# A decoder layer on one core: x for the head's factors in tiles of their own, and w_o's reloads on ScalarE's queue

## The chip, the cores and the metric

The kernel runs on one core of one Trainium2 chip. Work is shared by TensorE (PE in the profile: matmuls and transposes), VectorE (DVE), ScalarE (ACT), GpSimd (POOL, little used here) and SyncE (SP, which only issues DMAs). Each engine carries out its own instructions strictly in order, and waits at the first one whose input or buffer isn't ready. ScalarE can issue DMAs too; then the issue stands in the same order as its computations. The metric is the device time in microseconds (us). The kernel before takes 2449.53 us, the median of three runs (2446.66 to 2450.91).

## The reference

One hybrid decoder layer in float32 on 512 tokens of width 2048:

```python
h = rms_norm(x, g_mix)
z = h @ w_in          # attn q,k,v | ret q,k,v | ret gate, 8 heads of 128 each
a_out = moba_attention(rotary(rms(q)), rotary(rms(k)), v)       # 8 heads, causal
r = retention_chunkwise(rotary(rq), rotary(rk) * 128**-0.5, rv) # 8 heads, decay per head
r_out = silu(rg) * (r * rsqrt(mean(r*r) + eps)) * g_ret
x = x + concat(a_out, r_out) @ w_o
x = x + (silu(h2 @ w_gate) * (h2 @ w_up)) @ w_down              # h2 = rms_norm(x, g_ffn)
x = x + (p @ w_ple_proj) * sigmoid(rms_norm(x, g_ple) @ w_ple_gate + b)
```

## The kernel before

**Number format.** A float32 product is made of three matmuls on a high and a low part: `split` (L51) makes the high part with a copy on ScalarE (H, L54) and the low part with a subtraction on VectorE (L55); `mm3` (L61 to L64) multiplies high by high, high by low and low by high. Weights are split in the same way, into `wh` and `wl` (three buffers each), one unit of 256 rows by 512 columns at a time.

**Products of factors.** Most projections use seven products in place of eight (a Strassen-Winograd scheme, the order of L101 is 1, 5, 6, 3, 7, 2, 4). The weights' sums are made by VectorE (L70), and the other operand's sums, its factors, by `factors` (L155) or, in the head, by `first_factors` (L426). A product goes to one of the PSUM banks X, Y and Z (L125). A unit of a product is 12 matmuls of 512 columns, a product of four units 48.

**The head.** Chunks of x, transposed (128 rows by 512), are loaded by `h_chunk` (L420), multiplied by the gain on ScalarE (L423), and split into the tile `h`. With `h` PE first makes the plain projection of the first q/k pair (class `Plain`, eight units of 24 matmuls, each of which needs two chunks of h). It ends in four copies `z0` out of PSUM (L414). Meanwhile `first_factors(k)` loads two chunks of x again for each of eight k, and makes the sums t (L67) and their splits into the tiles of products 5, 6, 3 and 7. Then the products of the values and gates follow (`groups`, L461): product 1 goes to X, product 5 to Z, which `z0` has to empty first. Besides, 16 tiles `xn` of x are loaded for the sums of squares (`sq`, L486), which the first rms norm needs. The tiles x, xn, sq, z0 and zeros all take turns in four buffers with the tag "o". `beside(i)` (L468) says at which step each piece of this is asked for.

**The middle.** Eight pairs of heads follow: four of attention, four of retention. For a retention pair `qk_ret` (L674) projects q and k (eight units from `h`), copies the four results `zr` out of PSUM (L680), swaps their halves by two small DMAs each on ScalarE's queue (`mr`, L683 and L684), turns them (L686 to L688) and splits them into qkH and qkL. `retain` (L696) makes the heads' output, and `factors` its factors for w_o. These go to DRAM (`spill`, tensors s_mix), since the tiles for w_o take the place of `h`, which lives until the last projection. In the last step of the loop (L751) `h` is given back, the tiles s_o of products 1, 5, 6 and 3 are opened, and `back` (L744) reloads them from DRAM on SP's queue: nine transfers of 512 KB, three of 256 KB and one of 1.75 MB. Then come `retain` for the last pair, whose factors go straight to the tiles, and the projection of p (L782; four units of 24 matmuls, with copies `pp` out of PSUM, L790). It needs pT, which takes the buffer of the table ropeT, free after the last turn.

**What sets the order.** The code gives the order of calls, but the program is laid out by a scheduler which keeps a simulated clock and moves each engine's instructions against each other as far as data and buffers allow. Every DMA issue also takes one of eight completion semaphores in turn, and so waits for the DMA eight before it.

Of the kernel before, what the change touches and what calls it, by code (L numbers as in the profile page):

```python
# [10 lines left out]
F32 = mybir.dt.float32  # L11
F32R = mybir.dt.float32r
BF16 = mybir.dt.bfloat16
AF = mybir.ActivationFunctionType
# [3 lines left out]
P = 128  # L18
# [3 lines left out]
NC = D // P  # L22
NS = D // 512
HD = 128
NPAIR = 4
# [8 lines left out]
def layer_kernel(ctx, tc, x, xT, pT, g_mix, wqk, w_vg, qk_norm, g_ret, w_ow, g_ffn,  # L34
                 w_gu, w_dn, g_ple, w_pl, b_pg, w_pp,
                 ident_c, rope_c, ropeT_c, decay_c, mask_c, out):
    nc = tc.nc
    PSUM = bass.MemoryType.PSUM

    def pool(name, bufs=1, side="left", **kw):  # L40
        return tc.tile_pool(name=name, bufs=bufs, side=side, reuse_waits="tile", **kw)
# [9 lines left out]
    def split(H, L, src, scale=None):  # L51

        if scale is None:
            nc.scalar.activation(H, src, AF.Copy)  # L54
            nc.vector.tensor_tensor(L, src, H.bitcast(F32), op=ALU.subtract)  # L55
        else:
            nc.scalar.activation(H, src, AF.Copy, scale=scale)
            nc.vector.scalar_tensor_tensor(L, src, scale, H.bitcast(F32),
                                           op0=ALU.mult, op1=ALU.subtract)
# [6 lines left out]
    def sub(o, a, b):  # L66
        nc.vector.tensor_tensor(o, a, b, op=ALU.subtract)  # L67
# [7 lines left out]
    def rstd_of(ssq, r):  # L75

        nc.vector.tensor_reduce(r, ssq, axis=AX.X, op=ALU.add)
        nc.vector.tensor_scalar(r, r, 1.0 / D, EPS, op0=ALU.mult, op1=ALU.add)
        power(r, r, NB)
# [23 lines left out]
    def kept(name, n):  # L103
        return {p: dram.tile([P, n + 2 if p == "4" and n == 4 else n, 2, 256], F32R, name=f"{name}_{p}")
                for p in ORDER}

    KG = [8, 8, 6]
    s_mix = kept("mix", 8)
# [23 lines left out]
    pools = {}  # L132

    def later(n, fn):
        due.setdefault(now[0] + n, []).append(fn)
# [16 lines left out]
    def ev_tile(tag, bufs=2, shape=(P, T), name=None, dt=F32):  # L152
        return pools["ev"].tile(list(shape), dt, name=name or tag, tag=tag, bufs=bufs)

    def factors(a0, a1, sink):  # L155

        lo, hi = slice(0, 256), slice(256, 512)
        t = [ev_tile("t", 2, (P, 2, 256)) for _ in range(2)]
        s1, s2, s3, s4 = t[0][:, 0], t[0][:, 1], t[1][:, 0], t[1][:, 1]
        made = {"1": a0[:, lo], "5": s1, "6": s2, "3": s4, "7": s3, "2": a1[:, lo], "4": a1[:, hi]}  # L160
        first = {"5": lambda: sub(s1, a0[:, hi], a1[:, hi]), "6": lambda: sub(s2, a0[:, lo], s1),
                 "3": lambda: sub(s4, a1[:, lo], s2), "7": lambda: sub(s3, a1[:, hi], s2)}
        for p in ORDER:
            if p in first:
                first[p]()
            H, L, end = sink(p)
            split(H, L, made[p])
            end()

    def into(tiles, k):  # L170
        return lambda p: (tiles[p][:, k, 0, :], tiles[p][:, k, 1, :], lambda: None)

    def spill(where, k, wait=1):
        def sink(p):
            o = ev_tile("o", 4, (P, 2, 256), dt=F32R)
            store = lambda: nc.sync.dma_start(where[p][:, k].bitcast(F32), o.bitcast(F32))
            return o[:, 0, :], o[:, 1, :], lambda: later(wait, store) if wait else store()
        return sink

    def factor_tile(p):  # L180
        return pools.get("s" + p, pools["s"]).tile(
            [P, 8, 2, 256], F32R, name="s" + p, tag="s" + p)
# [177 lines left out]
    h_ctx = ctx.enter_context(ExitStack())  # L360
# [14 lines left out]

    zeros = ev_tile("o", 4, name="zeros", dt=BF16)
    nc.vector.memset(zeros, 0.0)
    idle = tp_p.tile([P, T], F32, name="tp", tag="tp")
    for _ in range(10):
        nc.tensor.matmul(idle, zeros[:, :P], zeros, start=True, stop=True)  # L380
# [36 lines left out]
    zd = [dram.tile([P, T], F32, name=f"z_{b}") for b in range(NB)]  # L417
    first = Plain()

    def h_chunk(k):  # L420
        t = ev_tile("o", 4, name="x")
        nc.sync.dma_start(t, xT[k * P:(k + 1) * P, :])
        nc.scalar.activation(t, t, AF.Copy, scale=gm[:, k:k + 1])  # L423
        return t

    def first_factors(k):  # L426

        a = [h_chunk(2 * k + c) for c in range(2)]
        lo, hi = slice(0, 256), slice(256, 512)
        t = [ev_tile("v", name="t", shape=(P, 2, 256)) for _ in range(2)]  # L430
        s1, s2, s3, s4 = t[0][:, 0], t[0][:, 1], t[1][:, 0], t[1][:, 1]
        sub(s1, a[0][:, hi], a[1][:, hi])
        sub(s2, a[0][:, lo], s1)
        split(s_h["5"][:, k, 0, :], s_h["5"][:, k, 1, :], s1)
        split(s_h["6"][:, k, 0, :], s_h["6"][:, k, 1, :], s2)
        sub(s4, a[1][:, lo], s2)
        sub(s3, a[1][:, hi], s2)
        split(s_h["3"][:, k, 0, :], s_h["3"][:, k, 1, :], s4)
        split(s_h["7"][:, k, 0, :], s_h["7"][:, k, 1, :], s3)
# [28 lines left out]
    def beside(i):  # L468

        if -2 <= i < NC // 2 - 2:  # L470
            for k in (2 * i + 4, 2 * i + 5):
                t = h_chunk(k)
                split(h[:, k, 0, :], h[:, k, 1, :], t)
            first.load(i + 2)
        if 3 <= i < 3 + NC // 2:
            first_factors(i - 3)
        for at, q in ((2, "11"), (3, "12"), (6, "22")):
            if i == at:
                for u in range(4):
                    groups[0].load(q, u)  # L480
        if 6 <= i < 22:
            b, s = divmod(i - 6, NS)
            t = ev_tile("o", 4, name="xn")
            nc.sync.dma_start(t, x[b * P:(b + 1) * P, s * T:(s + 1) * T])
            sq = ev_tile("o", 4, name="sq")
            nc.scalar.activation(sq, t, AF.Square, accum_out=ssq[0][:, b, s:s + 1])  # L486
        elif i == 22:
            rstd_of(ssq[0], rstd[0])

    run(beside)  # L490
    s_ctx.close()
    ev_ctx.close()
# [12 lines left out]
    def rm_tile(name, shape=(P, T), dt=F32):  # L505
        return ev2.tile(list(shape), dt, name=name, tag="rm", bufs=4)
# [52 lines left out]
    def load_ropeT():  # L559
        t = ap.tile([P, 2, T], F32, name="ropeT", tag="rope")  # L560
        nc.sync.dma_start(t, ropeT_c)
        bc = rp_tile("bc")
        nc.scalar.activation(bc, over_partitions(rstd1), AF.Copy)
        nc.vector.tensor_tensor(t, t, bc[:, None, :].to_broadcast([P, 2, T]), op=ALU.mult)
        tab[0] = t
# [6 lines left out]
    def v_of(i):  # L572
        v = ap.tile([P, NB, 2, 256], F32R, name="v", tag="v")
        j = i % NPAIR
        for b in range(NB):
            nc.sync.dma_start(v[:, b].bitcast(F32), vd[i // NPAIR][:, b, :, j * 256:(j + 1) * 256].bitcast(F32))
        return v
# [165 lines left out]

    def back(p, pairs):  # L744

        nc.sync.dma_start(s_o[p][:, pairs].bitcast(F32), s_mix[p][:, pairs].bitcast(F32))

    qk, v = qk_attn(0), v_of(0)
    s_o = {}
    for i in range(2 * NPAIR):  # L750
        if i + 1 == 2 * NPAIR:  # L751
            h_ctx.close()
            pools["s"] = ctx.enter_context(pool("s2"))
            s_o.update({p: factor_tile(p) for p in "1563"})
            for u in range(3):
                for p in "156":
                    back(p, slice(2 * u, 2 * u + 2))
            for p in "156":
                back(p, slice(6, 7))
            back("3", slice(0, 7))  # L760
        if i < NPAIR:
            made = [attend(qk, v, j) for j in range(2)]
        else:
            made = [retain(qk, v, j, 2 * (i - NPAIR) + j) for j in range(2)]
        spilled = spill(s_mix, i, 0)
        direct = into(s_o, i)
        factors(*made, lambda p: (direct if p in s_o else spilled)(p))
        if i + 1 < 2 * NPAIR:
            if i + 1 == NPAIR:
                load_ropeT()  # L770
            qk = qk_attn(i + 1) if i + 1 < NPAIR else qk_ret(i + 1)
            v = v_of(i + 1)


    pTH = []
# [6 lines left out]
    for n in range(NS):  # L782
        wh, wl = weights(w_pp[n])
        accs = [acc_p.tile([P, T], F32, name="acc", tag="acc") for _ in range(NB)]
        for b in range(NB):
            at = slice(b * P, (b + 1) * P)
            for c in range(2):
                mm3(accs[b], pTH[c][0][:, at], pTH[c][1][:, at], wh[:, c, :], wl[:, c, :], c == 0, c == 1)
            t = rm_tile("pp")
            nc.scalar.activation(t, accs[b], AF.Copy)  # L790
            nc.sync.dma_start(ppd[b][:, n], t)
    mix_ctx.close()


# [3 lines left out]
    pools["chain"] = ctx.enter_context(pool("chain2", space=PSUM))  # L798
    s_o.update({p: factor_tile(p) for p in "724"})
    for p in "724":  # L800
        back(p, slice(0, 8))

    s_c, s_e = {}, {}
    s_d = [{}, {}, {}]
# [35 lines left out]
    for kg in range(3):  # L840
        for n in range(2):
            after = lambda p: None
            if n == 1:
# [3 lines left out]
                                         lambda tb, s, kg=kg: xd[kg + 1][tb][:, s],  # L847
# [105 lines left out]
```

## Time and profile before

| | |
|---|---|
| time before | 2449.53 us (2446.66 to 2450.91) |
| profiled execution, device time | 2448.14 us |
| its span | 2446.4 us |
| PE busy | 2332.6 us (95%) |
| DVE busy | 1958.1 us (80%) |
| ACT busy | 1211.8 us (50%) |
| mean granted TensorE clock | 0.984 |

The span runs from the first to the last instruction of the trace; the device time holds 1.7 us more. A busy PE is not a PE at its peak, since matmuls overlap: at full clock one of 512 columns starts every 0.227 us and shows 0.39 us. The same holds on DVE and ACT, where the shown duration exceeds the distance of two that follow each other: a subtraction of 128x1024 takes 1.14 us so (shown 1.22), one of 128x512 0.60, one of 128x256 0.34; on ACT a copy of 128x512 about 0.52 to 0.62, one of 128x1024 0.95, one of 128x256 0.31.

### The profile page before, as it was taken

The numbers are of one execution on the slowest core, as the hardware profiler recorded it, in microseconds if no ns is written. First come the engines' busy times: TensorE is split into PE (matmuls) and PEld (weight loads), VectorE is DVE, ScalarE is ACT, GpSimd is POOL, SyncE is SP. The second block draws the span as 40 slices with busy tenths as digits, with TensorE's granted clock in tenths as the row PEclk, the third lists the DMA queues.
The fourth block names the chain that finished last, engine by engine and source line by source line (L and its number), as shares of the span: only waits on it lengthen the run. The fifth ranks groups of instructions, "written<-read, shape, count | busy, mean of one in ns | idle before, by whom it ended". The sixth has DMA issues, their size and how long they took to land.

```text
span 2446.4 us, 29405 instructions
## 1 busy us (share of the span) xinstructions
PE 2332.6 (95%) x10470; PEld 1911.5 (78%) x10470; DVE 1958.1 (80%) x2632; ACT 1211.8 (50%) x1886; POOL 62.4 (3%) x63
## 2 busy tenths in 40 slices
PE   8799999998986998999999999999999999999898
PEld 6578877787875876888888888888877878878677
DVE  5787767766566898798888988899878878789897
ACT  6654534444445465455445554455544434346543
POOL 0000011210000000000000000000000000000000
PEclk9899999999997999999999999999999999999999
DMA  7456453344567768444455444654595676767763
GB/s 277 140 187 206 151 163 116 117 134 141 171 190 251 265 203 308 137 147 128 135 186 176 138 128 156 194 155 132 172 397 180 249 282 209 295 235 242 260 213 121
DMA packets 170291, 469.91 MB, mean 192 GB/s; under 512 B 18848, under 2 KB 31520, under 8 KB 165152
## 3 DMA queue, kind: packets, MB, share of 16 engines
q1 hardware_dynamic: 167440, 463.82, 56.4%
q10 hardware_dynamic: 2704, 4.20, 0.7%
q8 instruction: 82, 1.34, 0.2%
q14 instruction: 65, 0.53, 0.1%
HBM read 357.33 MB, written 106.43 MB: 190 GB/s over the span
## 4 chain that ended last, share of the span: by engine, by line
PE 67%; DVE 10%; DMA 6%; issue 3%; ACT 1%; ACTq 0%; POOL 0%; SPq 0%; DVEq 0%
PE Y L63 8%; PE Y L64 8%; PE Y L62 8%; PE Z L63 5%; PE Z L64 5%; PE Z L62 5%; PE X L63 5%; PE X L64 5%; PE X L62 5%; PE acc L62 4%; PE acc L64 4%; PE acc L63 3%; DVE wl L55 3%; DVE raw L70 2%; DMA mr<-zr 1%
## 5 line engine op out<-in xcount | busy, mean ns | idle before, releaser
L54 ACT ACTIVATE wh<-raw 128x1024 fp32r<-128x1024 f32 x726 | 767.3, 1059 | 801.4 <-PE Y L64 283.2
L55 DVE TENSOR_TENSOR wl<-raw,wh 128x1024 fp32r<-128x1024 f32 x726 | 884.0, 1224 | 273.0 <-ACT wh L54 268.9
L70 DVE TENSOR_TENSOR raw<-raw 128x1024 f32<-128x1024 f32 x376 | 455.5, 1224 | 35.0 <-DMA raw<-in_w_gu 11.3
L63 PE MATMUL Y<-wl,s 128*128 128x512 f32 x1080 | 425.5, 394 | 3.4 <-DVE wl L55 3.2
L64 PE MATMUL Y<-wh,s 128*128 128x512 f32 x1080 | 421.8, 391 | 0.0
L62 PE MATMUL Y<-wh,s 128*128 128x512 f32 x1080 | 379.0, 391 | 9.7 <-ACT wh L54 9.7
L63 PE MATMUL Z<-wl,s 128*128 128x512 f32 x752 | 298.5, 397 | 6.6 <-DVE wl L55 6.6
L64 PE MATMUL Z<-wh,s 128*128 128x512 f32 x752 | 295.1, 393 | 0.0
L62 PE MATMUL Z<-wh,s 128*128 128x512 f32 x752 | 267.4, 395 | 19.6 <-ACT z L414 16.4
L63 PE MATMUL X<-wl,s 128*128 128x512 f32 x656 | 258.3, 394 | 5.9 <-DVE wl L55 5.6
L64 PE MATMUL X<-wh,s 128*128 128x512 f32 x656 | 256.3, 391 | 0.0
L62 PEld LDWEIGHTS Y<-wh,s 128*128 128x128 f32 x1080 | 202.1, 188 | 55.7 <-ACT wh L54 14.0
L63 PEld LDWEIGHTS Y<-wl,s 128*128 128x128 f32 x1080 | 203.3, 188 | 47.7 <-DVE wl L55 6.3
L64 PEld LDWEIGHTS Y<-wh,s 128*128 128x128 f32 x1080 | 203.4, 188 | 41.2
L62 PE MATMUL X<-wh,s 128*128 128x512 f32 x656 | 231.2, 392 | 2.3 <-ACT wh L54 2.3
L62 PEld LDWEIGHTS Z<-wh,s 128*128 128x128 f32 x752 | 141.5, 190 | 50.5 <-ACT z L414 16.8
L63 PEld LDWEIGHTS Z<-wl,s 128*128 128x128 f32 x752 | 142.7, 190 | 40.0 <-DVE wl L55 11.1
L64 PEld LDWEIGHTS Z<-wh,s 128*128 128x128 f32 x752 | 142.6, 190 | 28.8
L63 PEld LDWEIGHTS X<-wl,s 128*128 128x128 f32 x656 | 123.8, 189 | 34.4 <-DVE wl L55 8.9
L62 PEld LDWEIGHTS X<-wh,s 128*128 128x128 f32 x656 | 123.3, 189 | 29.5 <-ACT wh L54 3.9
L64 PEld LDWEIGHTS X<-wh,s 128*128 128x128 f32 x656 | 123.8, 189 | 25.3
L62 PE MATMUL acc<-h,wh 128*128 128x512 f32 x256 | 100.9, 397 | 6.0 <-ACT zr L680 4.0
(207 smaller groups left out, 2821.8 us busy)
## 6 DMA issues: line engine op xcount, KB each, us to landing
raw<-in_w_gu SPq DMA_DIRECT2D x176, 512.0 KB, 4.3
raw<-in_w_dn SPq DMA_DIRECT2D x88, 512.0 KB, 6.1
a<-o SPq DMA_DIRECT2D x154, 256.0 KB, 2.5
raw<-in_wqk SPq DMA_DIRECT2D x64, 512.0 KB, 3.9
s<-a SPq DMA_DIRECT2D x14, 2048.0 KB, 10.8
raw<-in_w_vg SPq DMA_DIRECT2D x48, 512.0 KB, 5.4
raw<-in_w_ow SPq DMA_DIRECT2D x32, 512.0 KB, 4.5
xin<-x SPq DMA_DIRECT2D x64, 256.0 KB, 6.0
```

The lines of the kernel that those rows point to most:

```text
L54: nc.scalar.activation(H, src, AF.Copy)
L55: nc.vector.tensor_tensor(L, src, H.bitcast(F32), op=ALU.subtract)
L62: nc.tensor.matmul(o, aH, bH, start=start, stop=False, skip_group_check=goes_on)
L63: nc.tensor.matmul(o, aH, bL, start=False, stop=False, skip_group_check=goes_on)
L64: nc.tensor.matmul(o, aL, bH, start=False, stop=stop, skip_group_check=goes_on)
L70: nc.vector.tensor_tensor(o, a, b, op=ALU.add)
```

## The change

Five edits:

1. A small activation `warm` on ScalarE reads `zeros` before the first x lands. It brings the table load of the first activation with it.
2. The chunks of x for `first_factors` come in tiles with the tags "e1" and "e5" (two buffers each), no longer in "o". These buffers are used only later by the products' copies.
3. `first_factors` is asked for one step earlier, the `xn` tiles one step later.
4. The last but one pair's factors are made after the last projection has been asked for (`mixed`), so that, like those of the last pair, they go straight to the tiles of products 1, 5, 6 and 3 where they had gone to DRAM and back.
5. `back` issues on ScalarE's queue. Its calls move from the last step of the pairs' loop into the loop of p's projection: three transfers after each of its first three units, and the one for product 3 after the fourth. The tiles of products 7, 2 and 4 are still loaded by SP, as before.

```diff
     nc.vector.memset(zeros, 0.0)
+    warm = ev_tile("v", name="warm")
+    nc.scalar.activation(warm[:, :P], zeros[:, :P], AF.Copy)
...
-    def h_chunk(k):
-        t = ev_tile("o", 4, name="x")
+    def h_chunk(k, tag="o", bufs=4):
+        t = ev_tile(tag, bufs, name="x")
...
-        a = [h_chunk(2 * k + c) for c in range(2)]
+        a = [h_chunk(2 * k + c, ("e1", "e5")[c], 2) for c in range(2)]
...
-        if 3 <= i < 3 + NC // 2:
-            first_factors(i - 3)
+        if 2 <= i < 2 + NC // 2:
+            first_factors(i - 2)
...
-        if 6 <= i < 22:
-            b, s = divmod(i - 6, NS)
+        if 7 <= i < 23:
+            b, s = divmod(i - 7, NS)
...
     def back(p, pairs):
-        nc.sync.dma_start(s_o[p][:, pairs].bitcast(F32), s_mix[p][:, pairs].bitcast(F32))
+        nc.scalar.dma_start(s_o[p][:, pairs].bitcast(F32), s_mix[p][:, pairs].bitcast(F32))
...
+    def mixed(i, made):
+        spilled = spill(s_mix, i, 0)
+        direct = into(s_o, i)
+        factors(*made, lambda p: (direct if p in s_o else spilled)(p))
     for i in range(2 * NPAIR):
-        if i + 1 == 2 * NPAIR:
-            h_ctx.close()
-            pools["s"] = ctx.enter_context(pool("s2"))
-            s_o.update({p: factor_tile(p) for p in "1563"})
-            for u in range(3):
-                for p in "156":
-                    back(p, slice(2 * u, 2 * u + 2))
-            for p in "156":
-                back(p, slice(6, 7))
-            back("3", slice(0, 7))
...
+        if i + 2 != 2 * NPAIR:
+            mixed(i, made)
...
+        if i + 2 == 2 * NPAIR:
+            h_ctx.close()
+            pools["s"] = ctx.enter_context(pool("s2"))
+            s_o.update({p: factor_tile(p) for p in "1563"})
+            mixed(i, made)
...
             nc.sync.dma_start(ppd[b][:, n], t)
+        for p in "156" if n < 3 else "3":
+            back(p, slice(2 * n, 2 * n + 2) if n < 3 else slice(0, 6))
```

The diff doesn't show where the scheduler puts these pieces. At three places it matters.

**SP's queue, the head's first loads**, before: from the weights of units 4 and 5 of `Plain` (in_wqk) to the eighth chunk of x for `h` (the last row; all x here are chunks for `h`).

```order
L390 DMA raw<-in_wqk 128x1024 x2
L422 DMA x<-in_xT 128x512
L204 DMA raw<-in_w_vg 128x1024
L422 DMA x<-in_xT 128x512
L204 DMA raw<-in_w_vg 128x1024 x3
L422 DMA x<-in_xT 128x512
L204 DMA raw<-in_w_vg 128x1024
L390 DMA raw<-in_wqk 128x1024
L204 DMA raw<-in_w_vg 128x1024
L390 DMA raw<-in_wqk 128x1024
L204 DMA raw<-in_w_vg 128x1024
L422 DMA x<-in_xT 128x512
```

The same queue now, from the weights of unit 4 on; of the four x in the second row two are for the factors, of the next three two, and the eighth chunk for `h` is the first of the last four.

```order
L392 DMA raw<-in_wqk 128x1024
L424 DMA x<-in_xT 128x512 x4
L392 DMA raw<-in_wqk 128x1024
L204 DMA raw<-in_w_vg 128x1024
L424 DMA x<-in_xT 128x512 x3
L204 DMA raw<-in_w_vg 128x1024 x6
L392 DMA raw<-in_wqk 128x1024 x2
L424 DMA x<-in_xT 128x512 x4
```

Four chunks of 256 KB for the factors have come to stand ahead of the eighth chunk for `h`.

**ScalarE, around the copies that empty `Plain`'s banks** (z<-Y, z<-Z), before: they stand behind the copies of x for the factors of k = 5 (the first row; those of k = 6 and 7 follow further down) and behind most of the splits (s<-t) of k = 4 and 5.

```order
L423 ACTIVATE x<-x,gm 128x512 x2
L54 ACTIVATE s_158<-t 128x256
L54 ACTIVATE s_159<-t 128x256
L54 ACTIVATE s_160<-t 128x256
L54 ACTIVATE s_161<-t 128x256
L486 ACTIVATE sq,ssq_80<-xn 128x512
L54 ACTIVATE s_158<-t 128x256
L414 ACTIVATE z_695<-Y_237 128x512
L414 ACTIVATE z_698<-Y_238 128x512
L54 ACTIVATE s_159<-t 128x256
L414 ACTIVATE z_701<-Z_239 128x512
```

Now: the last copies of x for the factors stand above, then the weights of product 1's third unit (wh), which need `Plain`'s last buffer, and the four copies follow.

```order
L425 ACTIVATE x<-x,gm 128x512
L54 ACTIVATE wh<-raw 128x1024
L54 ACTIVATE s_158<-t 128x256
L54 ACTIVATE s_159<-t 128x256
L416 ACTIVATE z_713<-Y_239 128x512
L416 ACTIVATE z_716<-Y_240 128x512
L416 ACTIVATE z_719<-Z_241 128x512
L416 ACTIVATE z_722<-Z_242 128x512
L54 ACTIVATE wh<-raw 128x1024
```

VectorE's row at this place, now, from the low part of that third unit's weights to that of the first unit of product 5:

```order
L55 TENSOR_TENSOR wl<-raw,wh 128x1024
L67 TENSOR_TENSOR t<-x,t 128x256 x2
L55 TENSOR_TENSOR s_158<-t,s_158 128x256
L55 TENSOR_TENSOR s_159<-t,s_159 128x256
L70 TENSOR_TENSOR raw<-raw 128x1024 x2
L55 TENSOR_TENSOR wl<-raw,wh 128x1024
L67 TENSOR_TENSOR t<-x 128x256
L55 TENSOR_TENSOR s_160<-t,s_160 128x256
L55 TENSOR_TENSOR s_161<-t,s_161 128x256
L55 TENSOR_TENSOR wl<-raw,wh 128x1024
```

Five instructions of 1024 columns and seven of 256 stand here; the next four units' rows follow in the same mixture.

**ScalarE, at the end of the last retention projection**, before: the four swaps (mr<-zr, two issues each) with the copies zr, the splits qkH, and the spilled factors (o).

```order
L683 DMA mr<-zr 64x512
L684 DMA mr<-zr 64x512
L680 ACTIVATE zr<-acc 128x512
L683 DMA mr<-zr 64x512
L684 DMA mr<-zr 64x512
L740 ACTIVATE r<-tp,gr 128x512
L54 ACTIVATE wh<-raw 128x1024
L54 ACTIVATE o<-t 128x256
L54 ACTIVATE qkH<-zr 128x512
L680 ACTIVATE zr<-acc 128x512
L54 ACTIVATE o<-t 128x256
L54 ACTIVATE qkH<-zr 128x512
```

Now, from the second issue of the second swap to the third swap (s_6314, s_6315, s_6316 and s_6317 are the tiles of products 1, 5, 6 and 3, mix_86 to mix_88 their factors in DRAM):

```order
L686 DMA mr<-zr 64x512
L54 ACTIVATE s_6314<-r 128x256
L748 DMA s_6314<-mix_86 128x1024
L54 ACTIVATE qkH<-zr 128x512
L682 ACTIVATE zr<-acc 128x512
L748 DMA s_6315<-mix_87 128x1024
L748 DMA s_6316<-mix_88 128x1024
L748 DMA s_6314<-mix_86 128x1024
L748 DMA s_6315<-mix_87 128x1024
L742 ACTIVATE r<-tp,gr 128x512
L685 DMA mr<-zr 64x512
L686 DMA mr<-zr 64x512
```

Five reloads have come to stand between the second and the third swap, and the other five, with one of 1.5 MB, between the third and the fourth; all ten stand ahead of the first matmul of p's projection.

## Rows read from the trace of the kernel before

**Rows 1.** The page: busy us (share of the span) and instructions by engine.

```profile
PE 2332.6 (95%) x10470; PEld 1911.5 (78%) x10470; DVE 1958.1 (80%) x2632; ACT 1211.8 (50%) x1886; POOL 62.4 (3%) x63
```

**Rows 2.** Windows of the head: length, busy time (instructions) by engine, clock, DMA share, GB/s.

```profile
10.00:20.00 10.00, 9.50 (x34) 7.72 (x35) 5.54 (x7) 7.13 (x11) 0.00 (x0) 1.00 1.03 410
35.00:40.00 5.00, 5.00 (x17) 3.99 (x16) 2.03 (x3) 3.27 (x6) 0.00 (x0) 0.71 0.62 231
...
75.00:80.00 5.00, 0.00 (x0) 0.00 (x0) 5.00 (x9) 1.33 (x2) 0.00 (x0) 0.55 0.36 105
90.00:95.00 5.00, 5.00 (x18) 4.01 (x17) 1.48 (x4) 2.71 (x7) 0.00 (x0) 0.75 0.52 184
```

**Rows 3.** Timeline of PE in the head: start, length, instruction, idle before and releaser.

```profile
33.51 0.50 PE L62 MATMUL Y<-wh,h 128*128 128x512 f32 x1 [2.01 <-ACT h L54]
70.42 0.39 PE L64 MATMUL X<-wh,h 128*128 128x512 f32 x1
87.17 0.80 PE L62 MATMUL Z<-wh,s 128*128 128x512 f32 x1 [16.36 <-ACT z L414]
113.10 0.62 PE L62 MATMUL Z<-wh,s 128*128 128x512 f32 x2
```

**Rows 4.** Timelines of ScalarE and SP in the head.

```profile
5.68 1.28 ACT L423 ACT_TABLE_LOAD   x1 [5.68 <-DMA x<-in_xT]
14.65 0.72 ACT L423 ACTIVATE x<-x,gm 128x512 f32<-128x512 f32 x1 [0.97 <-DMA x<-in_xT]
32.08 0.72 ACT L423 ACTIVATE x<-x,gm 128x512 f32<-128x512 f32 x1 [2.20 <-DMA x<-in_xT]
62.46 2.01 ACT L54 ACTIVATE wh<-raw 128x1024 fp32r<-128x1024 f32 x2 [0.97 <-PE Z L64]
85.27 1.06 ACT L414 ACTIVATE z<-Y 128x512 f32<-128x512 f32 x2
95.34 15.17 SPq L484 DMA_DIRECT2D xn<-in_x  x7
```

**Rows 5.** Windows in the middle, between the last two pairs; columns as in rows 2.

```profile
750.00:755.00 5.00, 2.62 (x7) 1.81 (x7) 4.37 (x9) 1.29 (x3) 0.00 (x0) 0.50 0.96 308
430.00:560.00 130.00, 123.66 (x599) 102.85 (x597) 90.60 (x223) 53.74 (x150) 23.64 (x23) 0.99 0.39 121
```

**Rows 6.** Waits, 690 to 800 us: who waited for whom, total us, times, longest.

```profile
PE at L62 <- ACT qkH L54: 24.9, 1, 24.9
ACT o L54 <- DMA mr<-zr: 7.1, 1, 7.1
```

**Rows 7.** Timelines of ScalarE and SP there, and of an earlier pair.

```profile
665.28 0.60 ACT L680 ACTIVATE zr<-acc 128x512 f32<-128x512 f32 x1 [0.55 <-PE acc L64]
686.59 0.63 ACT L54 ACTIVATE qkH<-zr 128x512 fp32r<-128x512 f32 x1 [0.18 <-DVE zr L688]
722.51 0.60 ACT L680 ACTIVATE zr<-acc 128x512 f32<-128x512 f32 x1 [0.27 <-PE acc L64]
726.59 8.58 SPq L746 DMA_DIRECT2D s<-mix  x10
738.73 0.47 ACTq L683 DMA_DIRECT2D mr<-zr  x1
751.24 0.63 ACT L54 ACTIVATE qkH<-zr 128x512 fp32r<-128x512 f32 x1 [2.04 <-DVE zr L688]
```

**Rows 8.** The chain that ended last, there: start, length, what.

```profile
724.99 6.88 DMA mr<-zr
731.90 9.31 DMA s<-mix
741.28 7.48 DMA mix<-o
```

**Rows 9.** DMA issues, 720 to 760 us: count, KB each, median us to landing.

```profile
s<-mix SPq DMA_DIRECT2D x9, 512.0 KB, 7.7
mr<-zr ACTq DMA_DIRECT2D x8, 128.0 KB, 6.2
```

More of the change, by code (lines that the diff above doesn't have):

```diff
@@ L486, in beside @@
             nc.scalar.activation(sq, t, AF.Square, accum_out=ssq[0][:, b, s:s + 1])
-        elif i == 22:
+        elif i == 23:
             rstd_of(ssq[0], rstd[0])
@@ L764, in layer_kernel @@
             made = [retain(qk, v, j, 2 * (i - NPAIR) + j) for j in range(2)]
-        spilled = spill(s_mix, i, 0)
-        direct = into(s_o, i)
-        factors(*made, lambda p: (direct if p in s_o else spilled)(p))
+        if i + 2 != 2 * NPAIR:
+            mixed(i, made)
         if i + 1 < 2 * NPAIR:
@@ L800, in layer_kernel @@
     for p in "724":
-        back(p, slice(0, 8))
+        nc.sync.dma_start(s_o[p].bitcast(F32), s_mix[p].bitcast(F32))
     s_c, s_e = {}, {}
```

## The prediction

> **What bounds the kernel now.** I read the page first, then the windows, to find where PE is not busy, and for each such place the waits and the timeline. PE is busy 95% of the span [rows 1], so a change can pay only where PE stands still. Two stretches stand out. In the head PE ends product 1 at 70.42 and opens product 5 at 87.17: 16.36 us, waiting for ScalarE's copies z0, which empty bank Z [rows 3]. They start at 85.27, though the weights that waited for the last matmuls of `Plain` went ahead at 62.46 [rows 4]: PE's result had been there 23 us. What came late was a buffer with the tag "o", which x of the factors shares, and those wait for VectorE, busy 5.00 of 5.00 us there [rows 2]. Then 18 matmuls run in 5 us where the full rate is 22, at a clock of 0.75, between the levels of 1.2 and 2.4 GHz [rows 2]. In the middle PE waits 24.9 us, once, for qkH of the last pair [rows 6]. The chain there is a swap of 6.88 us, reloads of 9.31 us, stores of factors of 7.48 us [rows 8]: ScalarE's third swap leaves at 738.73, 16 us after the first zr [rows 7], and ScalarE then stands 7.1 us behind a DMA [rows 6].
>
> **The change, part by part.**
>
> *Warm.* The table load of 1.28 us began only as the first x landed, at 5.68 [rows 4]; now it is over by then. I count nothing: the head's loads decide next, below. If they didn't, it would give 1.28.
>
> *x for the factors, earlier.* This moves loads. Up to the fourth chunk of h SP issues 3.0 MB, up to the eighth 9.5 MB; their copies start at 14.65 and 32.08 [rows 4]. So 6.5 MB take 17.43 us, 2.68 us per MB, and between them the transfers run at 410 GB/s [rows 2]: a stretch full of DMA, whose landings follow the order of issue. Now 1.0 MB more stands ahead of the eighth chunk, so it comes 2.7 us later. PE already waited 2.01 us for it [rows 3], so this wait grows to about 4.7, and `Plain` and product 1 end 2.7 us later: the latter at 70.8 + 2.7 = 73.5. The slow rate behind the gap (17 matmuls in 5 us at a clock of 0.71 [rows 2], 5 fewer than 22, or 1.1 us) may last longer; I add 1.
>
> *What the stall turns into.* z0 no longer waits for x of the factors: in ScalarE's new order the four copies follow the weights of product 1's third unit, which wait for `Plain`'s end (62.3 + 2.7 = 65.0). They are done by 69, before product 1 ends. So the wait for Z goes, and VectorE is late next. Its new order has, from that unit's low part (weights copied at 66.0) to product 5's first, five instructions of 1024 columns and seven of 256: 5 x 1.14 + 7 x 0.34 = 8.1 us, so product 5 opens at 74.1, not 87.17. To product 6's first weights ten and five more follow, 13.1 us, to 87.2, where PE alone would be at 74.1 + 10.9 (48 matmuls of 0.227) = 85.0. From there VectorE is ahead again, and product 3, which opened at 113.10 [rows 3], opens at 87.2 + 10.9 = 98.1: 15.0 us earlier.
>
> *xn one step later.* Seven loads of xn took 15.17 us [rows 4], 2.2 each. Fourteen follow z0 now: from about 70 to 101. Behind them, on VectorE in order, stands the sum of the squares, and behind it the weights of product 3's third unit, due at 103.5. With 3 us of VectorE's work between, PE may wait 1 to 2 us; I take 1. So the head gives 15 - 1 - 1 = 13. Its ends: 17, if the added loads don't hold up the eighth chunk; 7, if ScalarE, which has about 5.7 us of work per unit of `Plain` now (four chunks, two splits of h, four of factors, one of weights) against PE's 5.44, idles 1 us more per unit between VectorE's answers.
>
> *The reloads.* Written into the loop of p's projection, they are not paced by it: the order has all ten on ScalarE ahead of p's first matmul, five of them between the second and the third swap. The first two swaps leave before any reload, so I let VectorE begin their turns at 731.4, as before. Then three instructions of 0.60, qkH, zr: 734.5. Four issues of 0.47 each, as one of the swap took [rows 7], a copy of 0.6, and the third swap is out by 738.0, where its first half went at 738.73 and its second over a microsecond later. It lands behind four reloads of 0.5 MB on the same queue, issued from 734.5 on: 4 x 0.5 x 2.68 = 5.4 us, and 0.7 for itself, or at about 742; the turn takes it to 743.9. But ScalarE has, between that swap and qkH, five more issues (2.4), six quarter splits (1.9), weights (0.95), qkH and zr (1.0) and the fourth swap (1.0): 7.3 us, so qkH comes at 745.3, and PE starts at 746 where it started at 751.9: 6 us gained. The fourth swap lands behind another 3.5 MB at 752; pT, free after it, is ready at 756, where PE is back in full work at 762 in the trace: again 6.
>
> Its bounds: an earlier pair, without reloads, needs from its first zr (665.28) to the third qkH (686.59) 21.3 us; here it is 722.51 to 751.24, or 28.7 [rows 7]. So 7.4 us is about all that freeing the swaps can give, 9 with less work on ScalarE than in that pair. Below, it may give nothing or cost 2, if the swaps wait until all 6 MB have landed (728 + 6 x 2.68 = 744, turn and splits after it, and the fourth queued behind). I take 6.
>
> *Factors written to the tiles.* The last but one pair stores three parts in place of seven, and four pieces are not reloaded. The stores of 7.48 us in the chain [rows 8] go with it, and with them ScalarE's wait for a buffer that such a store still reads; the sum above has no such wait, so nothing is counted twice. The tiles must wait for the end of the last projection, but the first factor stood at that place before. All reloads land by 752, and w_o's first product begins over 20 us of p's projection later; without that cover each 0.5 MB would cost 1.3.
>
> *Elsewhere* the order changes only inside attention, 430 to 560 us, where PE idles 6.3 us in all [rows 5]. I take 0, between -3 and +3.
>
> Sum: 2448.14 - 13 - 6 = 2429.1 for the profiled execution, which lies 1.39 below the median; so 2430.5.
>
> **The rivals.**
>
> A: *the reloads eat their gain.* The Trainium skill ("DMA: Bandwidth & Descriptors", Issuing engines are not separate DMA queues) says that transfers run on the same 16 DMA engines and interleave whichever engine issues them, so that another queue saves only issue time. By it the moved reloads hold up the swaps as before; the trace agrees so far as 0.13 MB of swap took 6.2 us beside SP's reloads [rows 9]. Without that rule, from the rows: reloads and swaps still meet between 734 and 752, and now all are in one queue. Then the third qkH stays at 751, and the time is 2449.5 - 13 = 2436.5. Against it: the third swap is issued before five of the ten.
>
> B: *the factors' chain bounds the head.* ScalarE and VectorE wait for each other eight times over (x, t, s), one in front of the other's `Plain` work; then the head gives 7 and the time is 2436.5 too. For it: ScalarE is near PE's pace per unit; against: VectorE idles 3 us in that stretch in my count.
>
> C: *the head gives its full 17, the middle 9, attention 2*: 2421.5.
>
> D, slower: *ScalarE is blocked by its own DMA issues.* Each waits for the DMA eight before it, and 0.5 MB takes 7.7 us to land there [rows 9]. If each of the five issues between the third and the fourth swap waited so long, 38.5 us would stand before qkH: PE would start at about 746 + 38 = 784, 32 us later than now, and the time would be 2449.5 - 13 + 32 = 2468.5. It turns slower once these issues wait over 19 us (the 13 and the 6), 3.8 each. Against it: SP put out ten in 8.58 us [rows 7], so eight in flight suffice as long as few others take part.
>
> **How the numbers follow.** Forecast 0.55 (2425 to 2435); A 0.14, B 0.13, C 0.12, D 0.06. The predicted time is 2430. The range of 8 in 10 reaches 3.5 past A, B and C, the spread left by attention: 2418 to 2440. About 0.2%, 5 us, is what a measurement of this kernel can tell from no change. Slower by more: D, 0.05. Within 5 us: 0.03, where A and B come together and a little more is lost. Faster: 0.92.
>
> **What would show it.** Right: the wait PE on z0 gone, with small waits for VectorE's wl in product 5; a gap of 4 to 5 us near 33 us for the eighth chunk of h; product 3 opening near 98; the middle's one wait near 19 us in place of 24.9, the ten reloads on ScalarE's queue ahead of the fourth swap. Wrong: product 3 after 105; qkH of the last pair's third tile over 751 minus the head's 15 by less than 3 us, or later; new waits of over 5 us in attention or in w_o's first products.

## The result, and the profile after

The changed kernel took 2435.09 us (median of 4 runs, 2432.59 to 2440.81), the kernel before 2450.22 (2446.66 to 2452.89). The ratio is 0.9942, 95% interval 0.9920 to 0.9965. A second series, on another occasion, gave 0.9932 (0.9920 to 0.9945). The profiled execution took 2433.47 us, its span 2431.7, against 2448.14 and 2446.4: 14.7 us less. Forecast for it was 2429.1, with 13 from the head and 6 from the middle.

In the head the stall is gone. Waits of PE, 0 to 110 us (who waited for whom, total us, times, longest):

```profile
PE Y L62 <- ACT h L54: 5.3, 1, 5.3
PE Y L62 <- ACT wh L54: 4.2, 2, 3.8
PE Y L63 <- DVE wl L55: 1.1, 2, 0.5
```

The wait of 16.36 us for z [rows 3] is in no row any more; the wait for the eighth chunk of h has grown from 2.01 us to 5.34. (The 3.8 us of the second row is the wait for the first weights of all.) The timeline of PE gives the places:

```profile
36.20 0.79 PE L62 MATMUL Y<-wh,h 128*128 128x512 f32 x1 [5.34 <-ACT h L54]
71.76 0.62 PE L62 MATMUL Z<-wh,s 128*128 128x512 f32 x2
74.25 0.39 PE L64 MATMUL X<-wh,h 128*128 128x512 f32 x1
98.45 0.62 PE L62 MATMUL Z<-wh,s 128*128 128x512 f32 x2
```

These answer to 33.51, 87.17, 70.42 and 113.10 of [rows 3]. Product 1 ends 3.8 us later than before, product 5's first two matmuls stand 15.4 earlier (now before product 1's end; the others follow it, from 74.48), and product 3, at 98.45, opens 14.7 earlier. That is the whole difference of the two executions, had by 100 us. Two windows of the head agree, and a third, attention moved by the head's gain, shows no change against the 123.66 us and 0.99 of [rows 5] (columns as in [rows 2]):

```profile
35.00:40.00 5.00, 3.80 (x9) 3.02 (x10) 3.25 (x8) 4.92 (x10) 0.00 (x0) 0.50 1.04 399
75.00:80.00 5.00, 5.00 (x24) 4.14 (x23) 5.00 (x7) 3.71 (x9) 0.00 (x0) 1.00 0.49 140
415.30:545.30 130.00, 123.85 (x594) 102.57 (x594) 89.59 (x213) 53.60 (x157) 23.63 (x24) 0.99 0.39 120
```

Behind the longer gap PE runs at 1.2 GHz (9 matmuls in 3.80 us, where 17 stood); from 75 to 80 us, where it stood still, it works at 2.4.

In the middle, the waits from 690 to 790 us:

```profile
PE at L62 <- ACT qkH L54: 14.6, 2, 10.9
PE tp L740 <- DVE r L736: 5.2, 1, 5.2
DVE zr L688 <- DMA mr<-zr: 7.5, 3, 4.2
```

The one wait of 24.9 us [rows 6] has become three: 5.2 for the rows r of the last but one pair, 10.9 for qkH of the last pair's third tile, 3.7 for qkH of its fourth. Timelines of ScalarE and of PE:

```profile
708.98 0.60 ACT L682 ACTIVATE zr<-acc 128x512 f32<-128x512 f32 x1 [0.55 <-PE acc L64]
722.60 0.61 ACTq L686 DMA_DIRECT2D mr<-zr  x1
723.25 0.60 ACTq L748 DMA_DIRECT2D s<-mix  x1
730.01 0.56 ACTq L686 DMA_DIRECT2D mr<-zr  x1
732.14 0.63 ACT L54 ACTIVATE qkH<-zr 128x512 fp32r<-128x512 f32 x1 [4.36 <-DVE zr L690]
745.02 0.63 ACT L54 ACTIVATE qkH<-zr 128x512 fp32r<-128x512 f32 x1
```
```profile
732.82 0.79 PE L62 MATMUL at<-qkH 128*128 128x512 f32 x1 [10.88 <-ACT qkH L54]
745.70 0.80 PE L62 MATMUL at<-qkH 128*128 128x512 f32 x1 [3.71 <-ACT qkH L54]
```

From the first zr to the third qkH it is 23.2 us now and was 28.7 [rows 7]: 5.6 gained. But the fourth qkH comes 36.0 us after the first zr, where it came 31.1 (753.64 less 722.51). The chain of waits shows the swaps that lie between (start, length, what):

```profile
710.17 7.09 DMA mr<-zr
722.60 7.39 DMA mr<-zr
730.01 12.66 DMA mr<-zr
```

The last takes 12.66 us for 128 KB; the reloads stand ahead of it in ScalarE's queue. PE's clock pays a second time (windows):

```profile
740.00:745.00 5.00, 2.00 (x13) 1.79 (x12) 2.65 (x5) 1.83 (x10) 0.00 (x0) 0.84 0.92 309
745.00:750.00 5.00, 4.30 (x11) 3.52 (x12) 3.12 (x8) 1.69 (x5) 1.01 (x1) 0.50 0.15 45
750.00:755.00 5.00, 5.00 (x23) 4.10 (x22) 2.32 (x4) 2.18 (x5) 0.00 (x0) 0.88 0.00 0
```

The clock had risen by 741, fell with the idle time up to 745.7, and rose again after 750.

To see the stages at once, I take from windows of 2.5 us what PE lost: the idle time, plus the busy time multiplied by (1 - granted clock). The head ends with the last matmul of the first groups (312.2 us before), the middle runs from the last pair's first zr to w_o's first matmul. Idle + lost to the lower clock, us; the kernels below the second line are those of the experiments:

```
                        head        between      middle
before               27.6 + 4.3   21.6 +  3.2   26.0 + 4.3
after                14.0 + 2.5   19.5 +  8.7   20.9 + 6.6
after, once more     13.5 + 3.6   21.2 +  8.7   20.7 + 5.2
tags alone           14.7 + 5.4   19.0 +  5.8   25.0 + 4.5
head's edits alone   13.9 + 2.4   20.8 + 10.7   21.8 + 3.4
middle's edits alone 27.9 + 4.0   19.8 + 10.9   25.9 + 2.8
old tags             28.4 + 4.8   19.8 +  9.4   25.8 + 2.0
reloads held         13.7 + 5.5   19.2 +  8.4   21.7 + 4.7
p's half early, held 12.2 + 4.4   20.3 + 10.1   23.5 +10.7
six buffers          13.0 + 1.7   19.5 +  5.8   13.2 + 5.4
six buffers, held    14.5 + 4.3   21.1 +  7.7   20.5 + 7.3
```

From before to after: the head 15.4 less, between 3.4 more, the middle 2.8 less. The last is no gain in time. From the last pair's first zr to w_o's first matmul 66.8 us pass before (722.51 to 789.34) and 66.8 now (708.98 to 775.81): PE loses less in this stage, but has as much more to do in it.

```profile
789.34 0.40 PE L62 MATMUL X<-wh,s 128*128 128x512 f32 x1
775.81 0.40 PE L62 MATMUL X<-wh,s 128*128 128x512 f32 x1
```

### The profile page after: what moved, and what is told of

The parts are those of the page before. It is cut to its first block, busy times and chain, and to the rows that moved or that the text cites. A ratio compares the mean times of both kernels' runs of the same rounds, so it can differ in the third digit from the quotient of the medians.

```text
span 2431.7 us, 29377 instructions
## 1 busy us (share of the span) xinstructions
PE 2341.2 (96%) x10470; PEld 1917.1 (79%) x10470; DVE 1957.4 (80%) x2632; ACT 1210.1 (50%) x1887; POOL 61.8 (3%) x63
## 4 chain that ended last, share of the span: by engine, by line
PE 67%; DVE 9%; DMA 7%; issue 2%; ACT 2%; ACTq 0%; POOL 0%; SPq 0%; DVEq 0%; POOLq 0%
PE Y L63 8%; PE Y L64 8%; PE Y L62 8%; PE Z L63 5%; PE Z L64 5%; PE Z L62 5%; PE X L63 5%; PE X L62 5%; PE X L64 5%; PE acc L62 4%; PE acc L63 4%; PE acc L64 4%; DVE wl L55 3%; DVE raw L70 2%; DMA mr<-zr 2%
```

## The experiments

Ratios are to the kernel before, timed in the same series. Line numbers in a row are those of its own kernel.

**The head's edits alone** (before, with warm, the tags and the shifted steps; nothing of the middle).

> Before plus the three edits of the head alone (warm, x in tags e1 and e5, the shifted steps); reloads and factors of the last pairs as before. Both theories: product 3 opens at 98.5, as in the changed kernel. Theory T (the middle's two edits give next to nothing, because the fourth swap lands 12.7 us after its issue behind the reloads and PE waits a second time and then runs at the lower clock): the time is that of the changed kernel within 3 us, 2435 to 2438. Rival R (the middle gives its 6 us and the new order inside attention takes 4 to 6 back): 2441.

Measured: 2436.05 us, ratio 0.9933 (0.9919 to 0.9948), product 3 at 97.3. The head's edits bring all that the five together bring. The middle of this kernel is 64.7 us long, that of after 66.8; it loses 25.2 us, after 27.5. Its order differs from before's too, though no edit touches it, since the scheduler lays it out anew: the third qkH comes 25.1 us after the first zr (711.74), where it came 28.7 before and comes 23.2 in after.

```profile
736.87 0.63 ACT L54 ACTIVATE qkH<-zr 128x512 fp32r<-128x512 f32 x1 [5.51 <-DVE zr L690]
```

**The middle's edits alone** (edits 4 and 5: the factors of the last but one pair late, the reloads in p's loop on ScalarE).

> Before plus the two edits of the middle alone (last but one pair's factors after the projection, reloads on ScalarE's queue); head as before. T: 0 to 3 us below before, 2447 to 2450; PE waits for qkH twice, the second time some 4 us, with the clock at half for 5 us after it. R: 2444, since attention keeps its old order.

Measured: 2450.43 us, ratio 0.9997 (0.9989 to 1.0006): nothing. T's time was nearly right, its mechanism was not: there was no second long wait for qkH here, but one of 25.78 us, as long as before's. In this kernel's order all ten reloads stand ahead of the third swap, whose first half landed 13.69 us after its issue; the third qkH came 29.6 us after the first zr (725.66), no earlier than before. So the 5.6 us that after shows there are not what edits 4 and 5 give by themselves: they hang on the order that the scheduler made of all five.

```profile
755.24 0.63 ACT L54 ACTIVATE qkH<-zr 128x512 fp32r<-128x512 f32 x1 [13.30 <-DVE zr L688]
755.93 0.80 PE L62 MATMUL at<-qkH 128*128 128x512 f32 x1 [25.78 <-ACT qkH L54]
```

It also gives something else. Up to the last pair PE has the same instructions in the same order as before. Yet its granted clock there differs; windows of before, then of this kernel:

```profile
300.00:420.00 120.00, 115.77 (x543) 95.12 (x542) 81.61 (x168) 49.45 (x123) 23.27 (x23) 1.00 0.47 145
540.00:660.00 120.00, 109.68 (x538) 91.17 (x537) 75.96 (x149) 51.11 (x110) 3.02 (x3) 0.99 0.51 152
```
```profile
300.00:420.00 120.00, 115.72 (x530) 95.03 (x529) 80.79 (x167) 47.87 (x121) 22.20 (x22) 0.97 0.45 143
540.00:660.00 120.00, 111.87 (x535) 93.19 (x534) 75.27 (x150) 51.17 (x112) 3.02 (x3) 0.96 0.50 153
```

So up to 8 us of clock in the column "between" (3.2 against 10.9) come without a change in what PE is given to do, and after's 8.7 there can't be put down to an edit.

**The reloads on SP's queue again**, at their new place.

```diff
-        nc.scalar.dma_start(s_o[p][:, pairs].bitcast(F32), ...)
+        nc.sync.dma_start(s_o[p][:, pairs].bitcast(F32), ...)
```

> The changed kernel with the ten reloads on SP's queue again, at the same place of the program (after the loads of v, ahead of the swaps' third). If the order within ScalarE's queue is what holds up the fourth swap: it lands some 7 us after its issue in place of 12.7, the second wait for qkH (3.7 us) and the slow stretch after it (2.6 us) go, and the time is 2429 to 2431. If the bytes count and not the queue: the swaps land as late as in the changed kernel, 2434 to 2437.

Measured: 2437.06 us, ratio 0.9941 (0.9928 to 0.9953). Both expectations were half right: the swaps land early, as the first says, and the time is the second's. With the reloads in the other queue no swap took over 7.9 us to land (view of the tile mr; first line here, second after):

```profile
DMA to landing us min/median/max: 5.2/6.1/7.9
```
```profile
DMA to landing us min/median/max: 5.9/7.2/12.7
```

Both halves of the fourth swap landed while the last reload, issued 3.6 us ahead of the first half, was still under way (it took 13.7 us); in after they landed behind it. The wait of 3.7 us for the fourth qkH is gone, but PE idles 4.06 of the 5 us from 740 to 745 all the same (the window): its next matmul, at 744.20, writes to a bank that VectorE reads from 743.69 on, behind the turn of the fourth swap, and for p's work the chain has the load of p, which is there at 745.1, 34.2 us after the first zr, and so hardly earlier than in after (34.7):

```profile
740.00:745.00 5.00, 0.94 (x5) 0.83 (x5) 3.63 (x7) 0.00 (x0) 0.00 (x0) 0.50 0.90 345
```
```profile
736.93 8.19 DMA praw<-in_pT
```

The Trainium skill ("DMA: Bandwidth & Descriptors", Issuing engines are not separate DMA queues) says that a second issuing engine saves only the time of issuing. For the kernel's time the runs agree (0.9941 here, 0.9942 and 0.9932 for after); for a small transfer behind large ones this trace does not, 7.9 against 12.7 us.

**The reloads held** until the fourth qkH is there.

```diff
+    for p in "1563":
+        nc.scalar.activation(s_o[p][:, 0:6:2, 0, :1], qk[3][0][:, :3, None], AF.Copy)
```

> The changed kernel with the ten reloads held until qkH of the last pair's fourth tile is there (ScalarE writes three columns of each tile from it first, about 0.2 us each, which the reload overwrites). T: swaps land 4 us after their issue, the third qkH comes 2 to 4 us earlier than in the changed kernel, the fourth 8 to 10 us earlier, PE's second wait and the slow stretch after it go: 2427 to 2429. R: the middle has given its gain already, 2433 to 2436.

Measured: 2434.9 us, ratio 0.9935 (0.9923 to 0.9947), the rival's time. This refutes T. The fourth qkH does come 8.1 us earlier (736.94) and pT 9 us (736.40); PE has no second wait for qkH. Yet w_o's first matmul comes at 775.29, against 775.81 in the changed kernel. The windows tell where the time went:

```profile
750.00:755.00 5.00, 4.73 (x23) 3.62 (x22) 2.74 (x9) 2.44 (x10) 1.01 (x1) 1.00 1.06 431
755.00:760.00 5.00, 1.68 (x10) 1.30 (x11) 5.00 (x8) 2.36 (x5) 0.00 (x0) 0.99 1.00 388
760.00:765.00 5.00, 4.85 (x24) 4.29 (x23) 1.93 (x5) 3.22 (x10) 0.00 (x0) 0.67 0.63 239
```

Half of p's projection, begun some 10 us earlier, is done by 752.7; its other half stands behind the second head's scores in PE's order and begins at 763.45. In between PE waits for VectorE, which makes these scores' products (pt) and, busy 5.00 of 5.00, has weights of w_o between them:

```profile
755.86 0.55 DVE L713 TENSOR_TENSOR pt<-at,dec 128x384 f32<-128x384 f32 x1
756.93 1.22 DVE L70 TENSOR_TENSOR raw<-raw 128x1024 f32<-128x1024 f32 x1
```

**No warm** (that one activation taken out).

> The changed kernel without the early activation. If the loads decide what comes next (the prediction's 0): the first copy of x and PE's first matmul are 1.1 to 1.3 us later, the gap at the eighth chunk of h is that much shorter, product 3 opens at 98.5 as in the changed kernel, 2434 to 2437. Rival: all of the head is 1.1 us later.

Measured: 2435.75 us, ratio 0.9940 (0.9926 to 0.9954). PE's first matmul with weights begins at 10.74 in place of 9.42, but the gap at the eighth chunk ends at 36.81 (4.98 long) in place of 36.20, and product 3 opens at 97.8 in place of 98.45. The warm activation gives nothing that can be told, as forecast: half of the 1.3 us that it brings forward is gone at the eighth chunk, and all of it by product 3.

**No shift** (edit 3 undone).

```diff
-        if 2 <= i < 2 + NC // 2:
-            first_factors(i - 2)
+        if 3 <= i < 3 + NC // 2:
+            first_factors(i - 3)
...
```

> The changed kernel with the factors' x, and the loads of xn, at the steps of before; x keeps its own tags e1 and e5. If the tags are the cause of the stall of z0: that stall stays gone. The gap at the eighth chunk falls from 5.3 to 2 to 3 us (1 MB less ahead of it), but the factors' chain is a step (up to 5.4 us) later: product 3 opens at 98 to 102, 2435 to 2439. Rival (the shift is what brings the gain): product 5 opens at 80 or later, 2441 or more.

Measured: 2434.94 us, ratio 0.9949 (0.9934 to 0.9964); product 5 opens at 73.05, product 3 at 101.9. The tags suffice. The gap hardly shrank:

```profile
36.93 0.80 PE L62 MATMUL Y<-wh,h 128*128 128x512 f32 x1 [4.92 <-ACT h L54]
```

**Old tags** (the factors' x in "o" again, the steps shifted).

```diff
-        a = [h_chunk(2 * k + c, ("e1", "e5")[c], 2) for c in range(2)]
+        a = [h_chunk(2 * k + c) for c in range(2)]
```

> The changed kernel with the factors' x in buffers of tag o again; the steps stay shifted. If the shared buffers are the cause of the stall: PE waits for z0 again, 5 to 16 us, product 5 opens at 78 to 87, 2440 to 2450. Rival (the shift is what brings the gain): 2435.

Measured: 2450.8 us, ratio 1.0006 (0.9993 to 1.0019). The stall is back and with it all of the time; the gap at the eighth chunk is 1.76 us here, and no chunk for the factors is loaded ahead of that one.

```profile
88.25 0.79 PE L62 MATMUL Z<-wh,s 128*128 128x512 f32 x1 [17.83 <-ACT z L416]
```

**Half of p's projection ahead of the last pair's retention, reloads held.**

```diff
+    def p_part(ns):
+        H, L = weights(pT.rearrange("(k p) t -> p k t", p=P))
+        for n in ns:
+            ...
...
+        if i + 1 == 2 * NPAIR:
+            ...
+            p_part((0, 1))
...
+    p_part((2, 3))
```

> The changed kernel with the reloads held as in the kernel before this one, and two of the four parts of p's projection, whose weights and pT need nothing of the last pair, written ahead of the last pair's retention (pT is split into buffers of the weights, twice). Theory T2 (the middle is bounded by PE standing idle for the chain zr, swap, qkH while p's projection, which could fill it, comes behind it, so that what one wait gives back another takes): PE's idle and slow time in the middle falls from 27 us to 17 to 22, and the time to 2425 to 2431. Rival R2 (the middle's end is set by VectorE's work in order, not by PE's wait): it stays at 26 to 28 us, 2433 to 2437.

Measured: 2441.93 us (2432.19 to 2445.99), ratio 0.9959 (0.9944 to 0.9974), by its median slower than after, though the intervals touch. Both theories were wrong in the time and in the loss, which rose to 34.2 us. T2's remark that what one wait gives back another takes did hold: the first waits fell to 2.50, 2.63 and 2.89 us, and at the end, with p's work used up, two new ones stand in the second head:

```profile
772.25 0.58 PE L62 MATMUL at<-qkH 128*128 128x256 f32 x1 [4.08 <-DVE pt L713]
777.95 0.55 PE L724 MATMUL at<-v,PH 128*128 128x256 f32 x1 [4.05 <-DVE pt L713]
```

**The tags alone** (before, with edit 2 and nothing else).

> Before with one edit alone: the factors' x in tags e1 and e5 (no warm, no shifted steps, nothing in the middle). If that is the whole gain: 2435 to 2438. Rival (the other edits bring part of it): 2440 or more.

Measured: 2434.68 us, ratio 0.9946 (0.9933 to 0.9960). One edit of five is the gain; after, in the same series, had 0.9932 (0.9920 to 0.9945), so whether the other four add some 3 us or nothing can't be told.

```profile
71.34 0.62 PE L62 MATMUL Z<-wh,s 128*128 128x512 f32 x2
```

**After, once more.**

> The changed kernel once more, unaltered, to see how far two profiles of one order of instructions differ. If the lower clock inside attention is a matter of the execution and not of the order: PE's idle time by stage (14.0, 19.5, 20.9 us) comes again within 1 us, while its time at the lower clock inside attention (8.7 us) moves by several us. Otherwise both come again within 1 us.

Measured: 2432.44 us (2429.75 to 2434.10), ratio 0.9932. Idle times came again within 1.7 us, not within 1, and the loss to the clock between came again (8.7 and 8.7). But these two executions had the same mean granted clock, 0.983. Over the nine of this kernel it lay between 0.979 and 0.984, over twenty of before between 0.978 and 0.983: the clock of one program varies between executions, and two that agree don't show that its order fixes it. What decides stays open.

**Six buffers in place of four** for zr, mr, praw and pp, with pT in buffers of the weights, so that it need not wait for the last turn.

```diff
-        return ev2.tile(list(shape), dt, name=name, tag="rm", bufs=4)
+        return ev2.tile(list(shape), dt, name=name, tag="rm", bufs=6)
...
+    p_part((0, 1))
+    p_part((2, 3))
```

> The changed kernel with six buffers instead of four for zr, mr, praw and pp, and pT split into buffers of the weights (twice), which frees the room: the third zr need not wait for the first swap to be used, and pT not for the last rotation. If the chain zr, swap, qkH is what the middle's end hangs on: the third swap goes out by 716 us in place of 722.6, PE's wait of 10.9 us falls to 2 to 6, partly filled with p's projection, 2427 to 2431. If p's work only changes place (it is all that PE has besides the two heads, and what it covers early it leaves bare later, as in the two kernels with held reloads): 2433 to 2440.

Measured: 2424.91 us (5 runs, 2422.37 to 2429.71), ratio 0.9904 (0.9891 to 0.9917), the first expectation and more: 7.5 us below after in the same series, and so below before as well. The third zr now follows the second and its swap goes out 6.3 us after the first zr (13.1 in after, 16.2 in before); of PE's wait of 10.9 us for qkH none is left. The middle, from the first zr to w_o's first matmul, is 55.4 us long in place of 66.8. Timelines of ScalarE, then PE:

```profile
706.40 0.60 ACT L682 ACTIVATE zr<-acc 128x512 f32<-128x512 f32 x1 [0.25 <-PE acc L64]
710.05 0.60 ACT L682 ACTIVATE zr<-acc 128x512 f32<-128x512 f32 x1 [1.19 <-PE acc L64]
712.67 0.47 ACTq L685 DMA_DIRECT2D mr<-zr  x1
725.74 0.63 ACT L54 ACTIVATE qkH<-zr 128x512 fp32r<-128x512 f32 x1
737.02 0.63 ACT L54 ACTIVATE qkH<-zr 128x512 fp32r<-128x512 f32 x1 [0.30 <-DVE zr L690]
```
```profile
719.13 0.79 PE L62 MATMUL acc<-wh 128*128 128x512 f32 x1 [4.10 <-ACT zr L682]
724.19 0.80 PE L62 MATMUL acc<-wh 128*128 128x512 f32 x1 [2.14 <-ACT pp L787]
```

PE's longest waits are now for buffers of p's accumulators. The fourth qkH is nearly as late behind the third (11.3 us) as in after (12.9), and no wait of PE for it is left: p's work, which starts at 710 where it started at 747, stands in its place. Two things were changed here, the number of buffers and where pT is kept, and no run has one without the other; how the 7.5 us divide between them is not shown.

**Six buffers, reloads held.**

> As the kernel with six buffers, with the reloads held until the fourth qkH besides. If the chain counts: 2425 to 2429. If p's work only changes place: 2433 to 2440.

Measured: 2432.84 us, ratio 0.9937 (0.9923 to 0.9950), 8 us slower than without the hold; the first expectation is wrong. Held, the reloads begin at 734 us, and the stores of p's results, under way with them, give their buffers back late (chain of waits); ScalarE waits for those, 3.9 us at the longest, and for its own issues, 3.3, and makes the next weights late (PE's timeline):

```profile
734.02 9.42 DMA pp<-pp
```
```profile
752.46 2.07 PE L62 MATMUL acc<-wh 128*128 128x512 f32 x4 [8.04 <-ACT wh L54]
```

## Why the prediction was right in the head and wrong in the middle

*x for the factors: right, by sizes that cancel.* The cause, the shared buffer, is shown by two runs that differ from after and from before in it alone (1.0006 and 0.9946). Forecast was 98.1 for product 3's opening; 98.45 came. That it is so near is partly luck. Product 1 ended 1.1 us later than forecast, at 74.6; the gap was 5.34 us where 4.7 was forecast. Product 5 was to be held up by VectorE until 74.1: two of its matmuls ran at 71.76 and the others from 74.48, behind product 1, and none waited for VectorE. So product 6, but for two matmuls that ran ahead, came at 86.1 against 87.2, and took 12.3 us, not 10.9: the small waits for VectorE's wl, which the forecast had in product 5, came there. And what brought more bytes ahead of the eighth chunk is not the shifted step ("earlier" in the forecast's heading), but the free buffers, which let x of the factors be loaded as soon as it is asked for. Without the shift four such chunks still stand ahead, and the gap is 4.92 us; with the shift and the old buffers none does, and it is 1.76.

*xn and the clock: 1 us each too much.* The fourteen loads are issued from 68.54 to 96.2 (forecast 70 to 101), but no wait of over 0.5 us follows in product 3; and the head loses 2.5 us to the clock where before lost 4.3, since the second gap, with its own slow stretch, is gone. So the head gave 14.7 for 13.

*Warm: right at nothing* (0.9940 without it, 0.9942 and 0.9932 with it).

*The reloads: the step that failed.* The middle's 6 us did not come: the stage is 66.8 us long in both kernels, and the time lies within the forecast's range thanks to the head alone. (PE's three waits there add up to 19.8 us, near the 19 forecast for the one; the sum fits, the mechanism doesn't.) Two parts of the step came out: ten reloads ahead of the fourth swap, and the third qkH 5.6 us earlier against the first zr, 6 forecast. But the second is no proof of the mechanism: without edits 4 and 5 the new order brought 3.6 of it (25.1), and with them alone, or with them and without the shift, nothing (29.6 both times). What failed is "the fourth swap lands behind another 3.5 MB at 752; pT, free after it, is ready at 756 ... again 6". Measured from the first zr the swap was to land after 29.5 us and landed after 33.7 (730.01 + 12.66 less 708.98). PE waited again, and ran 5 us at half rate. That alone, however, is not the cause: with the fourth qkH 8 us earlier the time did not fall. The step's error is that it ends where PE starts. Between the last pair's projection and w_o PE has two heads, each a chain through ScalarE and VectorE, and besides the rest of the pair before only p's projection to put between. What an earlier start uses of it, or what stands too late in PE's order, is missing further on: so it went in the three kernels with held reloads. And a step of the chain that could be shortened was not named at all: the third zr waits for one of four buffers, and so for a whole swap and a turn.

*Factors written to the tiles:* not tried apart from the reloads; both together gave 0.9997.

*Elsewhere 0 between -3 and +3:* +3.4 by the table, of which idle time -2.1 and clock +5.5; kernels with one order of PE differ as much. In attention itself nothing changed (123.66 and 123.85 us busy of 130).

*The rivals.* A's time, 2436.5, was nearest (2435.1), and its sentence that reloads and swaps meet in one queue is what the trace shows; but the third qkH, which it let stay at 751, came early in this order, and the loss arose behind it. B's time is the same, but its cause is refuted (product 3 at 98.45); C has the head at most. D is refuted for this order: five issues between the third and the fourth swap cost ScalarE no wait like it. Waits of its kind do come where the reloads are held: 4.0 us with half of p's projection early, 3.3 with six buffers.

## What to carry to other kernels

Look for the buffer behind a stall: here one tag shared by two uses held up work whose operands had been ready for 23 us, and one line gave all of the gain, or all but some 3 us. Where a wait on a path is removed, add up what the engine does up to the next place where all paths join, since filler work that is used earlier is missing later; a gain at a stage's start is no gain at its end. A chain of transfers may be held by its buffers and not by the queue: clearing the queue around it brought nothing here (0.9935), two more buffers, with p's work put where PE had stood idle, 7.5 us. And an edit in one stage lets a scheduler lay out another anew, so that what a stage shows after two edits is not yet the work of either.

## What was not expected of the hardware

A transfer of 128 KB took 12.66 us from issue to landing behind reloads of 512 KB and 1.5 MB in its own queue (13.69 in the kernel with the middle's edits alone), and at most 7.9 us with them in another engine's queue, where it landed ahead of the last of them. And the same order of PE's instructions, in two executions of two kernels, ran at a mean granted clock of 1.00 and 0.97 from 300 to 420 us.
